# Retiming twelve attention units one by one, and four-block final products, in a hybrid decoder layer

## The chip, the cores and the metric

The kernel runs on one core of a Trainium2 chip. The metric is the device time of one execution in microseconds (us). PE is TensorE, which does the matmuls and turns tiles; DVE (VectorE), ACT (ScalarE) and POOL (GpSimd) do the elementwise work; SP (SyncE) issues most DMAs.

## The reference

One decoder layer on x of 1024 positions by 1024 channels in float32: a mixer of two parallel parts, and then a feed-forward part.

```python
h = rms_norm(x, ln_pre_mix)
proj = h @ w_in                            # 256 pool + 768 q + 768 k + 768 v channels
q, k = rope(q, pos), rope(k, pos)          # 12 heads of 64
pool_out = multi_scale_pool(u_pool, ...)   # window means over 2, 4, 8, 16 positions
attn_out = dilated_attention(q, k, v)      # windows (128,1), (512,4), (2048,16), merged by softmax weights
x = x + rms_norm(concat(pool_out, attn_out) @ w_out, ln_post_mix)
h = rms_norm(x, ln_pre_ffn)
f = (silu(h @ w_gate) * (h @ w_up)) @ w_down
x = x + rms_norm(f, ln_post_ffn)
```

## The kernel before, in words

Each float32 operand of a large product is split in a high part (written by ACT) and a low part, the difference (written by DVE or POOL), and multiplied in three passes. So each matmul operand that is computed on the chip costs an ACT copy and a subtraction. The program falls into three stages: projections, pool mixer and attention (up to about 430 us), then the output projection and the feed-forward part, which is done in seven Strassen-like products (430 to 1090), and its last product with the closing norm (1090 to 1167).

**Units.** Attention is done in six pairs of heads by two halves of the positions, h = 0 and 1, which gives twelve units, u0 to u11 (u0 to u7 are pairs 0 to 3, both halves in turn; u8 and u9 are h = 0 of pairs 4 and 5, u10 and u11 their h = 1). A unit has these steps:

- scores: PE multiplies q by k into a PSUM bank `ps_s`; DVE adds the mask and takes the row's minimum of the scaled scores (L554), ACT takes the exponent and its row sum (L557);
- join, in the function `join`: the two sides of the windows exchange row statistics. DVE forms `ex` for the sides A and B (L577), PE multiplies each by a selection matrix into another `ps_s`, and a row of small DVE steps (L583 to L597) ends in the weights `wv`;
- weighting: 16 multiplies of the exponents `pp` by `wv`, on DVE (L611) or POOL (L613) by the list `wd`;
- turns: PE turns the weighted exponents into `ps_t` (L116), ACT copies the high part `ptr` (L658), DVE subtracts the low part (L659). There are two buffers of `ptr`;
- products: PE multiplies `ptr` by v into `ps_o`; ACT and DVE (L693, L694, L623, L625) finish them into `mix`, which goes to DRAM in `mixd` (L630) and is loaded again as `m` for the output projection (L896).

**Fill.** While a unit's steps wait for DVE, ACT and POOL, PE gets matmuls of projections for later units in between: q and k of one half (`ps_pj`), or v. A finished q or k is rotated (`rope`, L315 to L325): DVE shuffles it (L320) and multiplies by the cosines (L321), an engine chosen by the table (`rq` for q, `rk` for k) multiplies by the sines (L322), another adds (L325), and ACT and DVE spread and split it (L344 to L352). Weights are split at L154 and L158, on DVE or POOL by the list `we`.

**What sets the order.** A step is put on a list with a place, a number in units (`put(steps, lo, hi)`): u + 0.62 is 62% of the way from the start of unit u to the next. A group of steps gets places spread evenly from lo to hi. `emit` sorts the list by place and writes the program in that order. Between those steps PE's matmuls stay in program order. DVE, ACT and POOL are ordered by a scheduler from the same program, with priority for the scores' and turns' helpers and double priority for the join, so their rows move with PE's. SP issues its DMAs in its queue's order, and a DMA that waits for data holds those behind it. The table `PRM` has the places: `h0` and `h1` for units of the two halves, `first` and `last` for u0 and u11, with s0 and s1 for the scores, m for the join, w0 and w1 for the weightings, t0 and t1 for the turns, v0 and v1 for the products. All units of the same half share their places.

**The end.** The class `End` closes the layer. When the last product's sums for all eight blocks of 128 channels are there, PE sums the squares over channels, POOL takes the power -1/2, and PE turns the result into one row factor `rb` in PSUM. Then DVE multiplies each block by the factor and the gain `g4s` (L1418, eight times), DVE or POOL adds the residual `xe` (L1422, eight times), and eight DMAs write 128 KB each.

## Time and profile before

| What | Value |
|---|---|
| median of 3 runs | 1167.78 us (1166.33 to 1168.17) |
| the profiled execution's own time | 1168.91 us |
| its span in the profile | 1167.1 us |
| PE busy | 1136.1 us, 97% of the span |
| DVE busy | 791.6 us, 68% |
| POOL busy | 608.9 us, 52% |
| ACT busy | 543.1 us, 47% |
| mean granted TensorE clock | 0.99 |

The span is the time between the first and the last recorded instruction of one execution; the execution's own time is 1.8 us longer. Busy shares are means over stages: DVE is far fuller in the attention stage than after it. A wait of PE is shown with the engine and line that released it.

### The profile page before, as it was taken

To read this page: it belongs to the slowest core of one execution; us is meant where nothing else is said; L and a number is where in the kernel's file an instruction comes from. 1 tells how busy PE (TensorE), PEld (TensorE's weight loads), DVE (VectorE), ACT (ScalarE), POOL (GpSimd) and SP (SyncE) were. 2 spreads that over 40 slices of the span, in tenths; PEclk is the share of its full clock that TensorE was granted. 3 is DMA by queue.
4 is the path that set the end of the run, shared out by engine and by line. 5 is a ranking of instruction groups with operands and counts; after the bars stand their busy time and mean duration, and the time that the engine had idled before them with its cause. 6 is when DMAs were issued, how large, how long until landed. Compare 5 with 4: busy or idle time off the path is not lost.

```text
span 1167.1 us, 17255 instructions
## 1 busy us (share of the span) xinstructions
PE 1136.1 (97%) x6134; PEld 980.1 (84%) x6134; DVE 791.6 (68%) x1477; ACT 543.1 (47%) x1033; POOL 608.9 (52%) x541
## 2 busy tenths in 40 slices
PE   8999999999998999999999999999999999999996
PEld 6998889989888888888888888888888888888896
DVE  7766778787887675779686665766565465454685
ACT  7356667666566575656433222232232435343420
POOL 0111546565555403160586667777675978656521
PEclk9999999999999999999999999999999999999998
DMA  7315151415124744732233545444535789666542
GB/s 271 102 60 181 37 181 37 159 59 181 55 73 152 281 162 145 280 118 99 87 143 145 185 155 206 163 171 174 188 139 190 266 292 322 207 210 191 178 144 72
DMA packets 85365, 188.51 MB, mean 162 GB/s; under 512 B 8736, under 2 KB 24352, under 8 KB 83872
## 3 DMA queue, kind: packets, MB, share of 16 engines
q1 hardware_dynamic: 84704, 186.90, 46.2%
q8 instruction: 48, 0.79, 0.3%
q10 hardware_dynamic: 576, 0.52, 0.1%
q14 instruction: 37, 0.30, 0.1%
HBM read 134.44 MB, written 52.95 MB: 161 GB/s over the span
## 4 chain that ended last, share of the span: by engine, by line
PE 80%; DVE 8%; ACT 4%; DMA 3%; issue 3%; POOL 1%; SPq 0%; ACTq 0%; POOLq 0%; DVEq 0%
PE ps_pj L113 28%; PE ps_o L113 22%; PE ps_s L113 20%; PE ps_t L113 8%; PE ps_t L116 2%; ACT pp L557 1%; DMA mixd<-mix 1%; DVE z L1041 1%; DVE z L1040 1%; DMA m<-mixd 1%; DMA b<-in_w_out_dram 1%; DVE k L345 1%; DVE whl L158 1%; ACT whl L154 1%; DMA xraw<-in_xT_dram 1%
## 5 line engine op out<-in xcount | busy, mean ns | idle before, releaser
L113 PE MATMUL ps_pj<-x,whl 128*128 128x512 f32 x480 | 145.9, 418 | 0.0
L1225 POOL TENSOR_TENSOR fw<-rw,fw 128x512 fp32r<-128x512 f32 x74 | 102.6, 1414 | 62.9 <-ACT fw L1223 62.9
L613 POOL TENSOR_SCALAR pp<-pp,wv 128x256 f32<-128x256 f32 (+1 forms) x156 | 72.0, 480 | 104.9 <-DVE wv L597 52.1
L113 PE MATMUL ps_o<-tT,fw 128*128 128x512 f32 x504 | 118.1, 390 | 0.0
L158 POOL TENSOR_TENSOR whl<-wraw,whl 128x512 fp32r<-128x512 f32 x50 | 66.5, 1350 | 90.4 <-ACT whl L154 61.0
L113 PEld LDWEIGHTS ps_o<-tT,fw 128*128 128x128 f32 x504 | 94.6, 188 | 20.3
L557 ACT ACTIVATE pp<-pp,sx 128x128 f32<-128x128 f32 (+1 forms) x192 | 89.3, 468 | 30.0 <-DVE sx L554 29.4
L113 PEld LDWEIGHTS ps_pj<-x,whl 128*128 128x128 f32 x480 | 87.4, 194 | 10.3 <-POOL whl L158 0.4
L1225 POOL TENSOR_TENSOR whl<-rw,whl 128x512 fp32r<-128x512 f32 x42 | 62.5, 1511 | 58.0 <-ACT whl L1223 58.0
L1223 ACT ACTIVATE fw<-rw 128x1024 fp32r<-128x1024 f32 x37 | 38.5, 1058 | 100.7 <-DVE rw L1191 42.4
L113 PE MATMUL ps_pj<-whl,x 128*128 128x256 f32 x528 | 80.3, 293 | 0.0
L1367 POOL TENSOR_TENSOR op<-rw,op 128x512 fp32r<-128x512 f32 x38 | 60.6, 1594 | 35.5 <-ACT op L1366 34.2
L659 DVE TENSOR_TENSOR ptr<-ps_t,ptr 128x512 fp32r<-128x512 f32 (+1 forms) x84 | 56.2, 669 | 26.4 <-ACT ptr L658 25.8
L113 PEld LDWEIGHTS ps_pj<-whl,x 128*128 128x128 f32 x528 | 70.7, 196 | 0.5 <-DVE whl L158 0.2
L322 POOL TENSOR_TENSOR rsw<-rsw,sinr 128x512 f32<-128x512 f32 x20 | 26.2, 1309 | 84.7 <-DVE rsw L320 84.7
L658 ACT ACTIVATE ptr<-ps_t 128x512 fp32r<-128x512 f32 (+1 forms) x84 | 48.4, 576 | 40.6 <-PE ps_t L116 39.4
L1366 ACT ACTIVATE op<-rw 128x1024 fp32r<-128x1024 f32 x38 | 40.2, 1060 | 56.3 <-PE ps_t L113 32.2
L113 PE MATMUL ps_o<-ptr,v 128*128 128x128 f32 (+1 forms) x472 | 58.6, 258 | 4.8 <-DVE ptr L659 4.8
L113 PE MATMUL ps_pj<-b,fw 128*128 128x512 f32 x264 | 62.3, 392 | 0.0
L113 PEld LDWEIGHTS ps_o<-ptr,v 128*128 128x128 f32 x472 | 52.6, 164 | 8.8 <-DVE ptr L659 5.9
L113 PEld LDWEIGHTS ps_pj<-b,fw 128*128 128x128 f32 x264 | 49.6, 188 | 10.9
L113 PE MATMUL ps_s<-k,qh 128*128 128x128 f32 (+1 forms) x192 | 53.6, 291 | 0.3 <-DVE sx L554 0.2
(302 smaller groups left out, 2914.9 us busy)
## 6 DMA issues: line engine op xcount, KB each, us to landing
rw<-bd SPq DMA_DIRECT2D x77, 256.0 KB, 4.5
v<-vd SPq DMA_DIRECT2D x22, 512.0 KB, 4.9
rw<-wsd SPq DMA_DIRECT2D x44, 256.0 KB, 4.0
rw<-in_w_gate_dram SPq DMA_DIRECT2D x20, 512.0 KB, 3.6
rw<-in_w_up_dram SPq DMA_DIRECT2D x20, 512.0 KB, 4.5
bd<-p SPq DMA_DIRECT2D x33, 256.0 KB, 2.9
rw<-in_w_down_dram SPq DMA_DIRECT2D x33, 256.0 KB, 4.4
fw<-in_w_down_dram SPq DMA_DIRECT2D x16, 512.0 KB, 4.1
```

The costliest lines, as they stand in the source:

```text
L113: return tc.keep_in_program_order(nc.tensor.matmul(*a, **k))
L116: return tc.keep_in_program_order(nc.tensor.transpose(dst, src, by))
L158: eng.tensor_tensor(dst[:, 1, at:at + w], src[:, at:at + w], dst[:, 0, at:at + w].bitcast(F32), ALU.subtract)
L322: eng[0].tensor_tensor(s, s, sinr[:, sl], ALU.mult)
L557: nc.scalar.activation(pt[:, j, lo:], pt[:, j, lo:], AF.Exp, bias=sx[:, 0, side, j, hd, 0:1], scale=-1.0, accum_out=sx[:, 0, side, j, hd, ...
L613: nc.gpsimd.tensor_scalar(pv, pv, un.wv[:, side, j, hd:hd + 1], 1.0, op0=ALU.mult, op1=ALU.mult)
L658: nc.scalar.activation(ptr[:, 0, :w], t[:, :w], AF.Copy)
L659: nc.vector.tensor_tensor(ptr[:, 1, :w], t[:, :w], ptr[:, 0, :w].bitcast(F32), ALU.subtract)
L1223: nc.scalar.activation(w[n][:, :, 0], raw[n], AF.Copy)
L1225: low[0] = nc.gpsimd.tensor_tensor(w[n][:, i, 1], raw[n][:, i], w[n][:, i, 0].bitcast(F32), ALU.subtract)
L1366: nc.scalar.activation(w[:, :, 0], raw, AF.Copy)
L1367: nc.gpsimd.tensor_tensor(w[:, 0, 1], raw[:, 0], w[:, 0, 0].bitcast(F32), ALU.subtract)
```

## The change

The table `PRM` gets new numbers throughout, and a new entry `du`: for each unit, offsets that are added to the places of its scores, join, weightings, turns and products. The work of the attention stage stays the same in kind and count, and PE issues the same matmuls, in another order. Four parts of the work go to another engine or another shape:

- `rk` moves the sine multiply of the ten k rotations in the fill from POOL to DVE, and `r0` moves one multiply of the first pair from DVE to POOL;
- `wd` puts one weighting more of each unit on DVE (4 in place of 3 of 16);
- `we` puts two weight splits on DVE that POOL did and one on POOL that DVE did;
- at the end, for the second half of positions, ACT multiplies each block of y by its gain `g4s` as soon as the block is summed. DVE then multiplies four blocks at once by the row factor (`times`), and two blocks at once get the residual (`plus`), the first two of them on POOL as two instructions. Four DMAs of 256 KB take the place of eight of 128 KB.

`dealt` with an empty `cut`, `pb` at 0 and `pe` at 1 change nothing here; `need` and `did` are assertions made while the program is written.

```diff
- 'we': (1, 1, 1, 0, 0, 0, 0, 0, 0, 0, 1, 1),
+ 'we': (0, 0, 0, 0, 0, 1, 0, 0, 0, 1, 1, 1),
- 'pm': (0.92, (0.78, 0, 0), (0.84, 1, 0), (0.99, 0, 1), (1.05, 1, 1)),
+ 'pm': (0.9242, (0.76, 0, 0), (0.85679, 1, 0), (1.02476, 0, 1), (1.05, 1, 1)),
- 'rk': (0, 0),
- 'r0': (1, 1),
+ 'rk': (1, 0),
+ 'r0': (0, 1),
- 'wd': (0, 1, 1, 0, 0, 0, 0, 0, 0, 0, 1, 0, 0, 0, 0, 0),
+ 'wd': (0, 1, 1, 0, 0, 0, 0, 1, 0, 1, 0, 0, 0, 0, 0, 0),
+ 'du': {...
+        1: {'t1': -0.0014, 'm': -0.0422, 's1': 0.0048, 'w0': -0.0401, 'v1': -0.0144},
...
@@ units
         g.update(**(G["first"] if u == 0 else {}), **(G["last"] if u == 11 else {}))
+        g.update({k: g[k] + d for k, d in G["du"].get(u, {}).items()})
@@ class End
+            if self.h:
+                nc.scalar.activation(src, src, AF.Copy, scale=g4s[:, d:d + 1])
...
             def add(d):
...
-                i = nc.vector.scalar_tensor_tensor(yd, yd, g4s[:, d:d + 1], box["rb"], op0=ALU.mult, op1=ALU.mult)
-                eng = nc.gpsimd if at_end and d in (0, 2, 4) else nc.vector
...
-                i = eng.tensor_tensor(yd, yd, self.x[d][:, lo:hi], ALU.add)
...
+            def times(n):
+                yd = yblock("%d2" % (n + 1))[:, :, lo:hi]
+                pin(nc.vector.tensor_tensor(yd, yd, box["rb"][:, None].to_broadcast([P, 4, hi - lo]), ALU.mult))
+            def plus(n, i, eng, queue, each):
+                yd, xd = yblock("%d2" % (n + 1))[:, i:i + 2, lo:hi], self.x4[n][:, i:i + 2, lo:hi]
+                for k in range(0, 2, each):
+                    o = eng.tensor_tensor(yd[:, k:k + each], yd[:, k:k + each], xd[:, k:k + each], ALU.add)
...
+                queue.dma_start(out[at:at + 2 * P, 512 + lo:512 + hi].rearrange("(d p) t -> p d t", p=P), yd)
...
+            sums = ((1, 0, nc.gpsimd, nc.scalar, 1), (1, 2, nc.vector, nc.sync, 2), (0, 0, nc.vector, nc.scalar, 2),
+                    (0, 2, nc.vector, nc.sync, 2))
```

The order in which DVE gets its instructions moves with the places. At the join of u1, before, DVE's order is as follows. `ps_o_1251` and `low_1335` belong to a product, `ps_pj_1229` to a projection, `ex` to the join, `ptr` to turns; L659, L694, L320, L321 and L577 are the lines named above.

```order
L659 TENSOR_TENSOR ptr_1317<-ps_t_1312,ptr_1317 128x512
L694 TENSOR_TENSOR ps_o_1251<-ps_o_1251,low_1335 64x512
L320 STREAM_SHUFFLE rsw_1348<-ps_pj_1229 128x512
L321 TENSOR_TENSOR rco_1349<-ps_pj_1229,cosr_271 128x512
L577 TENSOR_TENSOR ex_1377<-sx_1110,qdA_290 128x64
L659 TENSOR_TENSOR ptr_1365<-ps_t_1360,ptr_1365 128x512
L625 TENSOR_TENSOR mix_1252<-ps_o_1251,mix_1252 64x512
```

In the changed kernel, whose lines stand 30 further down in this part (L607 is the former L577, L724 the former L694), the same place reads:

```order
L689 TENSOR_TENSOR ptr_1318<-ps_t_1313,ptr_1318 128x512
L607 TENSOR_TENSOR ex_1364<-sx_1076,qdA_290 128x64
L350 STREAM_SHUFFLE rsw_1349<-ps_pj_1249 128x512
L351 TENSOR_TENSOR rco_1350<-ps_pj_1249,cosr_271 128x512
L724 TENSOR_TENSOR ps_o_1241<-ps_o_1241,low_1337 64x512
L613 TENSOR_TENSOR em_1370<-ps_s_1365,qdA_290 128x64
```

The join's second `ex` moved from behind three instructions of other work to ahead of them.

A little later, among the products of u1, DVE's order before is as follows. L351 and L352 spread the finished q of the fill.

```order
L554 ISA pp_1637,sx_1478<-ps_s_1656,mA_286 128x256
L554 ISA sx_1478 128x1
L351 CAST qh_1587<-rco_1589 64x512 x2
L577 TENSOR_TENSOR ex_1732<-sx_1478,qdB_292 128x64
L352 TENSOR_TENSOR ql1_95<-rco_1589,qh_1587 64x512 x2
L659 TENSOR_TENSOR ptr_1670<-ps_t_1665,ptr_1670 128x512
```

And in the changed kernel, with L381 and L382 for L351 and L352:

```order
L584 ISA pp_1641,sx_1476<-ps_s_1657,mA_286 128x256
L584 ISA sx_1476 128x1
L689 TENSOR_TENSOR ptr_1671<-ps_t_1666,ptr_1671 128x512
L724 TENSOR_TENSOR ps_o_1514<-ps_o_1514,low_1680 64x512
L607 TENSOR_TENSOR ex_1763<-sx_1476,qdA_290 128x64
L381 CAST qh_1589<-rco_1591 64x512 x2
L382 TENSOR_TENSOR ql1_95<-rco_1591,qh_1589 64x512 x2
```

The subtraction that makes the next `ptr` moved from behind the four instructions of L351 and L352 to ahead of them.

On SP, where the last of `mix` of the first half goes to DRAM and is loaded again, the order before is the following (`m02` and `m03` are the loads of `m`, `vd` is v on its way through DRAM, `wraw` a weight).

```order
L896 DMA m00_4546<-mixd_75 128x2x1024
L896 DMA m01_4548<-mixd_75 128x2x1024
L630 DMA mixd_75<-mix_4254 128x1024
L896 DMA m03_4575<-mixd_75 128x2x1024
L150 DMA wraw_4725<-in_w_out_dram 128x1024
L472 DMA vd_77<-vs_4531 128x2x512
L896 DMA m02_4581<-mixd_75 128x1024
```

In the changed kernel:

```order
L937 DMA m00_4533<-mixd_75 128x2x1024
L937 DMA m01_4535<-mixd_75 128x2x1024
L180 DMA wraw_4595<-in_w_out_dram 128x1024
L660 DMA mixd_75<-mix_4255 128x1024
L180 DMA wraw_4725<-in_w_out_dram 128x1024
L937 DMA m03_4576<-mixd_75 128x2x1024
L937 DMA m02_4574<-mixd_75 128x1024
L502 DMA vd_77<-vs_4550 128x2x512
```

The load `m02` moved ahead of the store `vd`, and one weight's load ahead of the store of `mix`.

## The prediction

> **What bounds the kernel now.** I read the page first, where PE has by far the largest share of the span, then the windows by stage, then PE's waits, and then the timeline at the longest of them. The windows' columns are the stretch, its length, busy time of PE, PEld, DVE, ACT and POOL (with instructions), the granted clock, the DMA share and GB/s.

> ```profile
> 100.00:430.00 330.00, 314.39 (x2092) 288.12 (x2091) 257.20 (x759) 212.92 (x571) 162.57 (x208) 0.98 0.37 123
> 430.00:1090.00 660.00, 659.68 (x2975) 544.08 (x2975) 413.34 (x491) 259.25 (x339) 410.09 (x290) 1.00 0.53 188
> 1090.00:1168.00 78.00, 66.05 (x434) 60.30 (x432) 52.95 (x90) 18.69 (x26) 21.12 (x17) 0.93 0.37 123
> ```

> PE bounds everything. Between 430 and 1090 us it idles 0.3 us, so nothing is to be had there. In the attention stage it idles 330.00 - 314.39 = 15.6 us, in the last stage 12. The matmuls stay the same ones, so the time can change only through these idle times and the clock. The attention's idle time has few owners:

> ```profile
> PE ps_o L113 <- DVE ptr L659: 4.8, 4, 1.5
> PE ps_s L113 <- DVE ex L577: 4.4, 3, 2.5
> PE ps_t L116 <- POOL pp L613: 3.0, 2, 2.7
> PE ps_pj L113 <- DMA m<-mixd: 2.2, 2, 1.6
> ```

> Each row is total, number and longest. PE waits for joins (`ex`), for turned weights (`ptr`), for weightings on POOL, and for `m`. There is a second price. After four of these waits come stretches at half clock. The one behind u1's join, and then a stretch of the same length that follows no wait:

> ```profile
> 122.70:126.10 3.40, 3.40 (x11) 2.64 (x10) 3.22 (x10) 1.98 (x4) 0.31 (x1) 0.50 0.00 0
> ...
> 140.00:143.40 3.40, 3.40 (x26) 3.40 (x26) 2.53 (x8) 3.35 (x10) 1.22 (x1) 1.00 0.11 43
> ```

> At clock 0.50, 3.4 us do the work of 1.7, so such a stretch costs about 1.7 us. The others lie behind the join at 305.84, the product at 342.81 and the turn at 374.45 (below).

> **The change part by part.**

> *Join of u1.* DVE first, then the join on PE and what POOL did at the time:

> ```profile
> 119.52 0.73 DVE L320 STREAM_SHUFFLE rsw<-ps_pj 128x512 f32<-128x512 f32 x1
> ...
> 120.15 0.66 DVE L321 TENSOR_TENSOR rco<-ps_pj,cosr 128x512 f32<-128x512 f32 x1
> ...
> 120.39 1.26 POOL L322 TENSOR_TENSOR rsw<-rsw,sinr 128x512 f32<-128x512 f32 x1 [8.93 <-DVE rsw L320]
> ...
> 120.74 0.99 DVE L577 TENSOR_TENSOR ex<-sx,qdA 128x64 f32<-128x64 f32 x1
> ...
> 121.78 0.43 PE L113 MATMUL ps_s<-ex,ls 128*128 128x64 f32 x2 [1.48 <-DVE ex L577]
> ```

> The second `ex` stands behind other work, and takes 0.99 us beside a POOL multiply. The order now puts it ahead of L320, L321 and L694, so DVE could do it from 119.5. PE has three matmuls of a projection fewer ahead of the join, so I leave 0.2 us of the wait: -1.3 (0.9 to 1.5). The half-clock stretch at 122.7 goes with it: -1.7 (0 to 1.7).

> *Products of u1, and one of u3.*

> ```profile
> 147.06 0.63 PE L113 MATMUL ps_o<-ptr,v 128*64 128x256 f32 x5 [0.42 <-DVE ptr L659]
> ...
> 147.71 1.12 DVE L351 CAST qh<-rco 64x512 fp32r<-64x512 f32 x2
> ...
> 149.01 1.40 DVE L352 TENSOR_TENSOR ql<-rco,qh 64x512 fp32r<-64x512 f32 x2
> ...
> 150.44 0.69 DVE L659 TENSOR_TENSOR ptr<-ps_t,ptr 128x512 fp32r<-128x512 f32 x1
> ...
> 151.19 0.79 PE L113 MATMUL ps_o<-ptr,v 128*64 128x128 f32 x7 [1.52 <-DVE ptr L659]
> ...
> 204.43 1.66 DVE L345 TENSOR_TENSOR k<-rcl,k 64x512 fp32r<-64x512 f32 x1
> ...
> 206.12 0.69 DVE L659 TENSOR_TENSOR ptr<-ps_t,ptr 128x512 fp32r<-128x512 f32 x1
> ...
> 206.87 0.33 PE L113 MATMUL ps_o<-ptr,v 128*64 128x256 f32 x1 [1.45 <-DVE ptr L659]
> ```

> In u1 PE idles 0.42 + 1.52 = 1.94 us, since `ptr` queues behind 2.5 us of q's spreading. The new order makes `ptr` first: -1.8. The products stand a little closer behind their turns now, so up to 0.5 of new waiting is the other end (-1.9 to +0.5). In u3, `ptr` stands behind the 1.66 us of L345; the new order spreads k well before: -1.3 of 1.45 (-1.45 to 0).

> *Join of u7.*

> ```profile
> 302.12 0.22 DVE L577 TENSOR_TENSOR ex<-sx,qdB 128x64 f32<-128x64 f32 x1
> ...
> 304.44 1.26 POOL L322 TENSOR_TENSOR rsw<-rsw,sinr 128x512 f32<-128x512 f32 x1 [6.19 <-DVE rsw L320]
> ...
> 304.78 1.00 DVE L577 TENSOR_TENSOR ex<-sx,qdA 128x64 f32<-128x64 f32 x1
> ...
> 305.84 0.43 PE L113 MATMUL ps_s<-ex,ls 128*128 128x64 f32 x2 [2.51 <-DVE ex L577]
> ```

> Here the second `ex` stays behind the same other work. What goes is the POOL multiply beside it, which is a k's and moves to DVE, behind. By the row of the other side, `ex` alone takes 0.22: 1.00 - 0.22 = -0.8. The remaining 1.7 us and the half-clock stretch stay. Ends: -4.2, wait and stretch both, to +0.5.

> At both joins `ex`, with two operands in SBUF, ends 0.08 us after POOL's multiply does (121.73 and 121.65; 305.78 and 305.70). [...]

> *Unchanged places.* The longest wait for `ptr` behind the small steps of u7's join (342.81), the join of u9, and the first turn of u9, which waits for POOL:

> ```profile
> 342.81 0.62 PE L113 MATMUL ps_o<-ptr,v 128*64 128x256 f32 x5 [1.39 <-DVE ptr L659]
> ...
> 374.45 0.68 PE L116 MATMUL ps_t<-idt,pp 128*128 128x128 f32 x4 [2.70 <-POOL pp L613]
> ```

> The first gets POOL's work sooner and DVE's later; I take 0 (-3.1 to +1.5). In the second POOL has one addition of a rotation (L325) more ahead of the weightings, and PE more matmuls ahead of the turn: +0.3, between -1.3 and +1.3, one POOL instruction like L322 below either way.

> *Pool means and the load of m.*

> ```profile
> 103.41 1.28 PE L113 MATMUL ps_o<-band,u 128*128 128x144 f32 x10 [0.95 <-DVE mix L627]
> ...
> 392.74 0.96 PE L113 MATMUL ps_pj<-m,whl 128*128 128x512 f32 x3 [0.54 <-DMA m<-mixd]
> ...
> 396.49 0.73 PE L113 MATMUL ps_pj<-m,whl 128*128 128x512 f32 x2 [1.65 <-DMA m<-mixd]
> ```

> The two `pool_means` come earlier and apart from the product that holds their bank: -0.7 (-0.95 to 0). On SP, `m02` no longer stands behind the store `vd`, but a weight's load came ahead of the store of `mix`: -1.0 (-2.2 to 0).

> *Work moved to DVE.* Its price by the rows of the attention stage, the last column before the bar being the count, then busy and mean ns:

> ```profile
> L322 POOL TENSOR_TENSOR rsw<-rsw,sinr 128x512 f32<-128x512 f32 x20 | 26.2, 1309 | 84.7 <-DVE rsw L320 84.7
> ...
> L321 DVE TENSOR_TENSOR rco<-ps_pj,cosr 128x512 f32<-128x512 f32 x20 | 13.5, 673 | 0.0
> ...
> L611 DVE TENSOR_SCALAR pp<-pp,wv 128x256 f32<-128x256 f32 x15 | 6.6, 481 | 0.2
> ...
> L158 DVE TENSOR_TENSOR whl<-wraw,whl 128x1024 fp32r<-128x1024 f32 x5 | 6.4, 1287 | 1.0 <-ACT whl L154 0.9
> ```

> No row shows the sine multiply on DVE. The bounds are L321 with 0.67 and the contended L345 with 1.66 us; POOL is busy in 162.57 of 330 us, half of the time, and loses this work itself, so I take 0.8. Ten of these, twelve weightings at 0.48 and one net split at 1.29 make 8 + 5.8 + 1.3 = 15 us (14 to 24). DVE goes from 257 to 272 of 330 us, 78% to 82%. It is no bound by share, but a fuller queue makes `ptr` and `ex` later, and some units' joins and products stand nearer behind their inputs than before. For such fresh waits I put +2.5, one like 1.5 us and a share of a half-clock stretch; ends 0 and +8, two like u7's join with a stretch each (2 x 4.2).

> *The end.*

> ```profile
> 1158.02 0.87 DVE L1418 SCALAR_TENSOR_TENSOR y<-y,g4s,ps_pj 128x256 f32<-128x256 f32 x2 [1.56 <-PE ps_pj L116]
> ...
> 1163.86 0.42 DVE L1422 TENSOR_TENSOR y<-y,xe 128x256 f32<-128x256 f32 x1
> ...
> L1441 DVE TENSOR_TENSOR y<-ps_o,y 128x512 f32<-128x512 f32 x3 | 1.9, 675 | 0.0
> ...
> L1422 DVE TENSOR_TENSOR y<-y,xe 128x512 f32<-128x512 f32 x8 | 8.9, 1162 | 0.0
> ```

> DVE works from 1158.02 to 1164.28. A sum over 128x512 with one PSUM operand takes 0.675, so I estimate 1.2 for `times` over 128x1024; two of these and three `plus` of 128x512 at 0.68 make 2.4 + 2.0 = 4.4 us against 6.26, -1.8. The ACT scaling falls beside the sums. A last transfer of twice the size gives back some 0.2: -1.6. At worst the three `plus` take the 1.16 of such sums in the first half, 1.4 more in all, and the transfer 0.7 more: +0.5. At best a `times` takes no more than two of the present multiplies (0.87): -1.6 - 2 x 0.33 - 0.2, about -2.5.

> *Sum.* -1.3 - 1.7 - 1.8 - 1.3 - 0.8 + 0 + 0.3 - 0.7 - 1.0 + 2.5 - 1.6 = -7.4. The profiled execution took 1168.9 us, 1.1 more than the median, so it would take 1161.5 now, and a median run 1160.4.

> [...]

> **The rivals.**

> *Every long wait goes.* Each unit's own places could also clear u7's and u9's waits with their three stretches: 1.7 + 1.4 + 2.7 + 3 x 1.7 = 10.9 less, and no fresh wait, 1160.4 - 10.9 = 1149.5, or about 1151 with part of the fresh ones. Against it: at u7's join DVE's order is the same.

> *DVE becomes the bound of the joins and products.* The ten sine multiplies read two SBUF operands, as L345 and `ex` do, which took 1.66 and 1.00 beside POOL. If each meets a split or a sum on POOL, DVE's extra work is 24 us, and `ptr` comes late. It decides once DVE's queue ahead of `ptr` is over 1 us longer in some four units. Four more waits of 1.5 with a stretch of 1.7 each are 12.8 in place of 2.5, and the 3.1 of u1's and u3's products don't come: 1160.4 + 10.3 + 3.1 = 1173.8. For it: DVE is 78% busy, and PE's waits for DVE are the largest now. Against it: POOL gives up as many instructions as DVE gets, and so meets fewer of DVE's others. [...]

> *The waits only move.* Each wait that goes comes back in another unit: only the end's gain is left with some of `m`, 1167.8 - 1.6 = 1166.2. For it: PE's matmuls between the steps are the same number, so a unit that gets more cover takes it from another.

> **How the numbers follow.** About 0.2%, 2.3 us, is what a measurement can tell from no change: 1165.4 to 1170.1. Forecast (1156 to 1165) 0.47, every wait gone 0.14, waits only move 0.20, of which a third gains more than 0.2%, DVE the bound 0.19. Faster is 0.47 + 0.14 + 0.07 = 0.68, the same 0.13, slower 0.19. The range for 8 in 10 runs from 1151 to 1171, which leaves out most of the DVE rival and part of the best one; the forecast's own is 1156 to 1165.

> **What would show it.** In the changed profile: no wait of over 0.5 us for `ex` near 120 and no half clock behind it; no wait for `ptr` near 150 and 206; a wait of about 1.7 for `ex` near 304 with `ex` at 0.2; the end's DVE work about 4.4 us. DVE in the attention stage near 272 us. It is wrong if waits for `ptr` and `ex` together are over 9 us again, or there are more than three half-clock stretches.

## The result, and the profile after

The changed kernel takes 1153.73 us, the median of 4 runs (1153.31 to 1156.6), against 1167.05 us for the kernel before in 4 runs (1165.22 to 1168.17): 13.3 us less, a ratio of 0.9893 with a 95% interval of 0.9871 to 0.9914. The profiled execution took 1153.31 us; its span is 1151.4, against 1167.1 before.

So the time lies 2.3 us below the forecast's own range of 1156 to 1165, inside the wide one of 1151 to 1171, and above the rival in which every long wait goes (1149.5 to 1151).

The windows by stage of the changed kernel (columns as in the prediction). Its attention stage ends 14.6 us earlier, so the cuts stand at 415.4 and 1075.4 where they stood at 430 and 1090:

```profile
100.00:415.40 315.40, 308.01 (x2087) 284.31 (x2087) 261.42 (x776) 213.65 (x566) 140.86 (x184) 0.99 0.37 129
415.40:1075.40 660.00, 659.18 (x2972) 543.81 (x2971) 415.20 (x492) 259.99 (x339) 410.58 (x289) 1.00 0.53 188
1075.40:1152.00 76.60, 65.79 (x434) 60.20 (x432) 50.36 (x72) 25.52 (x38) 20.46 (x16) 0.95 0.38 125
```

In the attention stage PE idles 7.4 us in place of 15.6, although DVE is busy for 261 of 315 us (83%) in place of 257 of 330 (78%). PE's waits of the changed kernel (L607 was L577, L643 was L613, L689 was L659, L584 was L554):

```profile
PE ps_t L146 <- POOL pp L643: 3.7, 3, 3.0
...
PE ps_s L143 <- DVE ex L607: 1.5, 1, 1.5
...
PE ps_o L143 <- DVE ptr L689: 1.3, 3, 0.6
...
PE ps_s L143 <- DVE sx L584: 0.3, 1, 0.3
PE ps_pj L143 <- POOL whl L188: 0.3, 1, 0.3
```

The wait for `m` has no row any more, and neither has u1's join, where both `ex` now end ahead of PE's need (the second waits for ACT itself):

```profile
117.12 0.23 DVE L607 TENSOR_TENSOR ex<-sx,qdA 128x64 f32<-128x64 f32 x1 [0.30 <-ACT pp L587]
...
117.98 0.55 PE L143 MATMUL ps_s<-ex,ls 128*128 128x64 f32 x4
```

One wait for `ex`, u7's, and one for the weighting in u9 are left of the long ones:

```profile
297.31 0.43 PE L143 MATMUL ps_s<-ex,ls 128*128 128x64 f32 x2 [1.55 <-DVE ex L607]
...
363.49 0.68 PE L146 MATMUL ps_t<-idt,pp 128*128 128x128 f32 x4 [3.00 <-POOL pp L643]
```

u9's wait has the pattern that u7's last product had before (shown below, where the prediction is gone through): on DVE the join's small steps are slow beside POOL's work (`wv` takes 0.90 us, against 0.17 at u7's last product, at 332.29), and on POOL a split and a rotation's addition (L355) stand ahead of the weighting.

```profile
361.00 0.90 DVE L627 TENSOR_TENSOR wv<-nm,dd 128x16 f32<-128x16 f32 x1
...
359.36 2.51 POOL L188 TENSOR_TENSOR whl<-wraw,whl 128x512 fp32r<-128x512 f32 x2
...
361.82 1.26 POOL L355 TENSOR_TENSOR rco<-rco,rsw 128x512 f32<-128x512 f32 x1
```

Of the four half-clock stretches in the attention stage one is left, behind the wait of u9; the place behind u1's join now runs at full clock:

```profile
365.40:368.80 3.40, 3.40 (x18) 3.40 (x18) 3.31 (x9) 0.89 (x4) 3.40 (x7) 0.50 0.99 398
122.70:126.10 3.40, 3.40 (x18) 2.56 (x17) 3.20 (x11) 0.93 (x3) 0.79 (x2) 1.00 0.00 0
```

At the end DVE's work is 4.5 us, where it was 6.3:

```profile
1143.10 2.35 DVE L1469 TENSOR_TENSOR y<-y,ps_pj 128x1024 f32<-128x1024 f32 x2 [1.30 <-PE ps_pj L146]
1145.37 2.24 DVE L1474 TENSOR_TENSOR y<-y,xe 128x512 f32<-128x512 f32 x3
```

### The profile page after: what moved, and what is told of

Its sections match the earlier page's. It is cut to its first block, busy times and chain, and to the rows that moved or that the text cites. A ratio compares the mean times of both kernels' runs of the same rounds, so it can differ in the third digit from the quotient of the medians.

```text
span 1151.4 us, 17214 instructions
## 1 busy us (share of the span) xinstructions
PE 1128.8 (98%) x6134; PEld 976.3 (85%) x6134; DVE 795.2 (69%) x1481; ACT 552.5 (48%) x1045; POOL 589.8 (51%) x517
## 3 DMA queue, kind: packets, MB, share of 16 engines
HBM read 134.44 MB, written 52.95 MB: 163 GB/s over the span
## 5 line engine op out<-in xcount | busy, mean ns | idle before, releaser
L143 PE MATMUL ps_pj<-x,whl 128*128 128x512 f32 x480 | 142.0, 409 | 0.0
L643 POOL TENSOR_SCALAR pp<-pp,wv 128x256 f32<-128x256 f32 (+1 forms) x144 | 69.8, 503 | 118.2 <-DVE wv L627 70.2
L188 POOL TENSOR_TENSOR whl<-wraw,whl 128x512 fp32r<-128x512 f32 x48 | 63.8, 1349 | 59.5 <-ACT whl L184 54.9
L689 DVE TENSOR_TENSOR ptr<-ps_t,ptr 128x512 fp32r<-128x512 f32 (+1 forms) x84 | 56.0, 666 | 13.7 <-ACT ptr L688 13.1
L143 PEld LDWEIGHTS ps_pj<-b,fw 128*128 128x128 f32 x264 | 49.6, 188 | 10.9
L143 PE MATMUL ps_s<-k,ql 128*128 128x128 f32 (+1 forms) x192 | 52.9, 284 | 0.0
```

Of the source, the lines that this page charges most:

```text
L143: return tc.keep_in_program_order(nc.tensor.matmul(*a, **k))
L188: eng.tensor_tensor(dst[:, 1, at:at + w], src[:, at:at + w], dst[:, 0, at:at + w].bitcast(F32), ALU.subtract)
L643: nc.gpsimd.tensor_scalar(pv, pv, un.wv[:, side, j, hd:hd + 1], 1.0, op0=ALU.mult, op1=ALU.mult)
L689: nc.vector.tensor_tensor(ptr[:, 1, :w], t[:, :w], ptr[:, 0, :w].bitcast(F32), ALU.subtract)
```

## Experiments

Theory: the gain is one of order. PE's long waits came from other work standing ahead of the instruction it waited for, on DVE and POOL, and the new places turn these orders round. Rivals: moving work off POOL brings it by itself; or the closing part does; or the common numbers do it and the single units' offsets are small corrections. The kernels ran in four groups, each beside the kernel before on the same chip; its medians there were 1166.43, 1167.13, 1166.65 and 1166.62 us, and the ratios below are to these. A part taken out of the changed kernel also upsets the order that the other numbers were made for, so what a part is worth depends on the rest: such differences don't add up.

**The parts alone and taken away.** `tail_only` is the kernel before with the new class `End`.

> The kernel before with the new closing class alone (gain on ScalarE, times, plus, four DMAs). If the closing part is worth what the two traces show from the last sum of y to the end (12.65 us before, 11.55 after), the time falls by 1.1 us, to about 1166.0. By the prediction's own term it falls by 1.6, to 1165.4. If the end is hidden by something else, nothing changes.

Measured: 1166.38 us in 11 runs, ratio 0.9999 (0.9991 to 1.0008). `old_tail` is the opposite, the changed kernel with the old `End`.

> The changed kernel with the closing part of before. If the new closing part is worth the 1.1 us that the traces show: 1154.8. If, as the run of it alone had it, it is worth nothing: 1153.7.

Measured: 1154.86 us (1154.65 to 1158.82), ratio 0.9907 (0.9892 to 0.9922), 1.1 us above the changed kernel, but the intervals of the two overlap. The profiles agree with each other: from the wait for the last `p` to the end of the span there are 11.7 us before (1155.44 to 1167.1), 11.4 in `old_tail` (1141.64 to 1153.0), 10.7 in `tail_only` (1153.90 to 1164.6) and 10.6 after (1140.78 to 1151.4). So the closing part is worth some 0.7 to 1.0 us of span, which the times can't settle. Of the larger figure 0.26 us is clock: in the profile of before alone the turn of the row factor (1157.29) fell into half clock and took 0.69 us, against 0.43 in the three others.

`engines_only` is the kernel before with the engine choices, at the old places.

```diff
-        'we': (1, 1, 1, 0, 0, 0, 0, 0, 0, 0, 1, 1),
+        'we': (0, 0, 0, 0, 0, 1, 0, 0, 0, 1, 1, 1),
-        'rk': (0, 0),
-        'r0': (1, 1),
+        'rk': (1, 0),
+        'r0': (0, 1),
-        'wd': (0, 1, 1, 0, 0, 0, 0, 0, 0, 0, 1, 0, 0, 0, 0, 0),
+        'wd': (0, 1, 1, 0, 0, 0, 0, 1, 0, 1, 0, 0, 0, 0, 0, 0),
```

> The kernel before with the engine choices alone (rk, r0, wd, we), all places old. Theory 'order': the gain comes from the places, so the moved work by itself gives at most the 0.8 us at u7's join and costs new waits for ptr and ex behind a fuller DVE queue: 1166 to 1171 us. Rival 'POOL relieved': most of the gain comes from GpSimd leaving VectorE's operands alone: 1157 to 1161 us, with two or three of the four half-clock stretches gone.

Measured: 1166.59 us in 12 runs, ratio 1.0004 (0.9994 to 1.0014), as the theory had it: POOL's relief alone brings nothing. At u7's join `ex` takes 0.21 us and PE waits 1.73, 0.8 less than before:

```profile
305.52 0.21 DVE L577 TENSOR_TENSOR ex<-sx,qdA 128x64 f32<-128x64 f32 x1
...
305.79 0.43 PE L113 MATMUL ps_s<-ex,ls 128*128 128x64 f32 x2 [1.73 <-DVE ex L577]
```

The waits for `ptr` fall too, from 4.8 to 1.3 us. But new waits for weightings and for scores (2.4 us, from 0.2) stand elsewhere, and in all PE still idles 13.9 us in the attention stage. The rows of the weightings:

```profile
PE ps_t L116 <- POOL pp L613: 4.3, 3, 2.7
...
PE ps_t L116 <- DVE pp L611: 1.8, 4, 0.7
```

`order_only` is the changed kernel with the four old engine choices.

> The changed kernel with the old engine choices (rk, r0, wd, we): new places, du and closing part only. Theory 'order': most of the gain stays, 1155 to 1159 us; the join of u7 waits 2.4 instead of 1.55 us and its half-clock stretch is back. Rival 'POOL relieved': 1162 us or more.

Measured: 1158.11 us (1155.93 to 1160.33), ratio 0.9936 (0.9924 to 0.9949). Of the 13.3 us, 8.3 remain without any of the moved work. Its profile has u7's wait at 2.33 us, as expected, but without the half-clock stretch that was expected too, and waits for `ptr` of 3.5 us in all against 1.3:

```profile
298.81 0.43 PE L143 MATMUL ps_s<-ex,ls 128*128 128x64 f32 x2 [2.33 <-DVE ex L607]
...
PE ps_o L143 <- DVE ptr L689: 3.5, 4, 1.6
```

Two of the four choices, undone singly in the changed kernel, tell which matters. `rk_back` sets `'rk': (0, 0)`:

> The changed kernel with the ten sine multiplies of k back on POOL. Theory 'POOL's instruction beside the join's ex was in the way': u7's join waits about 2.4 instead of 1.55 us and gets its half-clock stretch in most runs, 1156 to 1158 us. Rival 'the multiply only loads DVE' (the prediction's slower case): 1151 to 1153 us, since DVE loses 8 us of work.

Measured: 1159.28 us (1159.01 to 1160.95), ratio 0.9935 (0.9923 to 0.9947), 1 us more than expected: undoing this one choice costs as much as undoing all four. u7's join waits 2.31 us there, with a half-clock stretch (mean clock of the profile 0.993, against 0.995 in the changed kernel), and waits for `ptr` are 4.4 us in all. `wd_back` puts the old weighting list in:

> The changed kernel with the old list of weightings on DVE, one fewer per unit. If the weighting list matters by POOL's time before the first turns: u9's wait stays at 3.0, others appear for POOL, 1154.5 to 1157 us. If it only loads DVE: 1152 to 1153.5 us.

Measured: 1154.19 us (1154.06 to 1154.28), ratio 0.9888 (0.9876 to 0.9901). It lies between the two expectations, and the interval holds the changed kernel's ratio: no difference is shown. u9's wait is 3.00 us there too.

**More on DVE.** `rq_dve` goes on in the same direction, and puts q's ten sine multiplies on DVE too.

```diff
- 'rq': (0, 0),
+ 'rq': (1, 0),
```

> The changed kernel with q's ten sine multiplies on DVE too (rq like rk). If POOL's instructions beside DVE's are what makes DVE late, u9's join loses its collision with the multiply (small steps of 0.9 and 1.2 us there fall to 0.2), and the time falls to 1150 to 1153 us. If DVE's own load is what matters (the prediction's slower rival, now with 16 + 8 us more than before the change): 1155 us or more, with new waits for ptr.

Measured: 1176.82 us (1175.75 to 1179.32), ratio 1.0088 (1.0074 to 1.0102). So this is where the prediction's slower rival lies, one step further. But not in its way: PE hardly waits for `ptr` (0.6 us in all), it waits for weightings on POOL. The first theory missed as well: u9's small steps still take 1.25 and 1.17 us, now beside the split and the addition that POOL keeps, and the wait there is 3.19 us.

```profile
PE ps_t L146 <- POOL pp L643: 17.9, 5, 4.8
```

One of them on DVE, POOL and PE:

```profile
126.27 0.25 DVE L625 RECIPROCAL nm<-nm 128x16 f32<-128x16 f32 x1
126.50 0.69 DVE L724 TENSOR_TENSOR ps_o<-ps_o,low 64x512 f32<-64x512 f32 x1
127.12 0.72 DVE L350 STREAM_SHUFFLE rsw<-ps_pj 128x512 f32<-128x512 f32 x1
127.74 0.67 DVE L351 TENSOR_TENSOR rco<-ps_pj,cosr 128x512 f32<-128x512 f32 x1
128.33 0.66 DVE L627 TENSOR_TENSOR wv<-nm,dd 128x16 f32<-128x16 f32 x1
...
127.69 3.02 POOL L188 TENSOR_TENSOR whl<-wraw,whl 128x512 fp32r<-128x512 f32 x2 [5.49 <-ACT whl L184]
130.69 1.49 POOL L643 TENSOR_SCALAR pp<-pp,wv 128x256 f32<-128x256 f32 x3
...
131.26 1.12 PE L146 MATMUL ps_t<-idt,pp 128*128 128x128 f32 x4 [4.74 <-POOL pp L643]
```

The join's last step `wv` stands behind a product and a rotation (L724, L350, L351), and on POOL a weight split of 3.0 us stands ahead of the weightings. In the changed kernel `wv` comes right behind the reciprocal there, and POOL's split behind the weightings.

**The places.** `no_du` is the changed kernel with `'du': {}`.

> The changed kernel with du empty: all units of a half share their places again, with the new common numbers. If the single units' offsets carry the gain: 1160 to 1166 us, waits for ex and ptr of over 1 us back in three or more units. If the common numbers and the engine choices carry it: 1154 to 1157 us.

Measured: 1170.82 us (1168.39 to 1174.67), ratio 1.0042 (1.0028 to 1.0056). The offsets, some of a few thousandths of a unit, are worth 17 us, more than the whole change, and 5 more than the first expectation allowed. The waits that come back are not those expected: PE waits 13.7 us in all for weightings on POOL, twice 4.66 (L620 is the weighting there, L165 the split).

```profile
PE ps_t L123 <- POOL pp L620: 13.7, 5, 4.7
...
187.08 1.22 DVE L604 TENSOR_TENSOR wv<-nm,dd 128x16 f32<-128x16 f32 x1
...
187.01 2.49 POOL L165 TENSOR_TENSOR whl<-wraw,whl 128x512 fp32r<-128x512 f32 x2 [5.02 <-ACT whl L161]
...
190.44 1.32 PE L123 MATMUL ps_t<-idt,pp 128*128 128x128 f32 x4 [4.66 <-POOL pp L620]
```

It is the same picture as in `rq_dve`: on DVE `wv` behind a shuffle and a multiply of a rotation, on POOL the split first and the weightings behind it. `du_2_4` keeps only the offsets of u2 and u4, where the two waits are.

> The changed kernel with the offsets of u2 and u4 alone. Without any offsets PE waited 4.66 us twice for POOL's weightings, in u2 and u4, with half-clock stretches behind both. If the offsets work place by place, these two waits go with their 1.7 us each (and a further stretch): 1170.8 - 2 x 6.4 = 1158 us, the waits of the other units staying as without offsets. If the offsets work only as a whole: 1165 us or more.

Measured: 1160.78 us (1158.94 to 1163.85), ratio 0.9949 (0.9933 to 0.9965). So the offsets mostly work place by place: the two waits shrink to pairs of 0.78 and 0.72 to 0.73 us, and those of the other units (1.73 at u7's join, 3.46 in u9) are as without offsets. `two_v0` keeps only two numbers, the places of the products in these units, which turn POOL's order there round.

```diff
+ 'du': {2: {'v0': 0.0155}, 4: {'v0': 0.0085}},
```

> The changed kernel with only two of the offsets left: the products of u2 start 0.0155 units later and those of u4 0.0085 units later; these alone turn GpSimd's order there round, from weight split before weightings to weightings before weight split. Theory 'the order of a split and the weightings on GpSimd makes the two waits of 4.66 us': both go with their half-clock stretches, 1158 to 1161 us, as with all offsets of u2 and u4 (1160.8). Rival 'the offsets act by the cover they give PE's waits': so small a shift does little, 1168 us or more.

Measured: 1162.92 us (1160.33 to 1164.06), ratio 0.9971 (0.9959 to 0.9983), 2 us more than expected, but 7.9 below `no_du`. The order in `two_v0` at the first of the two places (the weighting is L546 there, the split L91, `wv` L530; the window ends in the split):

```profile
184.46 0.15 DVE L530 TENSOR_TENSOR wv<-nm,dd 128x16 f32<-128x16 f32 x1
...
184.79 6.12 POOL L546 TENSOR_SCALAR pp<-pp,wv 128x256 f32<-128x256 f32 x12 [4.29 <-DVE wv L530]
190.87 1.28 POOL L91 TENSOR_TENSOR whl<-wraw,whl 128x512 fp32r<-128x512 f32 x1
```

The weightings come first, and the two waits of 4.66 are two pairs of 0.84 and 0.72 and of 0.79 and 0.72. So these two places are shown as the cause of the two waits. They act on two queues, though: on DVE `wv` now comes ahead of the rotation and takes 0.15 us in place of 1.22, and on POOL the weightings come ahead of the split. How much of the 4.66 us each is worth was not separated.

`old_common` is the opposite of `no_du`: offsets, engines and closing part new, the common numbers old.

> The changed kernel with the old common numbers of places; offsets du, engine choices and closing part are the new ones. If the offsets alone carry the order's gain: 1154 to 1157 us. If offsets and common numbers only work together: 1161 us or more, with waits for POOL's weightings or DVE's ptr of over 1 us in three or more units.

Measured: 1167.63 us in 11 runs, ratio 1.0005 (0.9995 to 1.0016). The offsets only work on the numbers they were made for; a wait of 2.14 us for `ex` stands at u1's join, and POOL's weightings cost 5.2 us.

**An attempt on the wait that is left.** `u9_late` moves u9's first turns and products later, so that more matmuls lie between its join and its first turn.

```diff
-        9: {'m': 0.0183, 'w1': -0.0315, 't1': -0.0102, 's1': -0.0286},
+        9: {'m': 0.0183, 'w1': -0.0315, 't1': -0.0102, 's1': -0.0286, 't0': 0.25, 'v0': 0.1},
```

> The changed kernel with u9's first turns 0.25 units and its first products 0.1 units later, so that some 3 us more matmuls lie between u9's join and its first turn. Theory 'a wait costs itself and, when it fills enough of a 3.4 us window, a half-clock stretch': the 3.0 us wait for the weighting on POOL goes, and with it the only stretch in the attention stage: 3.0 + 1.7 less, about 1149 us, mean clock 0.997 or more in most runs. Rival 'the wait moves on': u9's products or u10's join wait instead, 1152 to 1154 us.

Measured: 1156.3 us (1152.77 to 1158.46), ratio 0.9904 (0.9889 to 0.992). The rival was right, and the result a little worse than it said. The wait is gone and comes back at u10's scores, 1.19 and 2.60 us, where PE needs a `ps_s` that DVE has not read yet (L487 is the former L554):

```profile
369.93 0.39 PE L46 MATMUL ps_s<-k,qh 128*128 128x256 f32 x1 [1.19 <-DVE sx L487]
...
373.70 0.57 PE L46 MATMUL ps_s<-k,qh 128*128 128x256 f32 x1 [2.60 <-DVE sx L487]
```

My reading is that DVE is behind by those 3 us here, whichever wait shows it; no run shows this by itself. No kernel tried beats the changed one.

## Why the prediction was right, and where its size was off

The direction, most places of the gain and the wide range held; the fall was 13.3 us where 7.4 were summed up, 1.8 times as much, and the time fell below the forecast's own range. The signs named for it held: no long wait at u1's join and products, 1.55 us at u7's with `ex` at 0.22, DVE's closing work at 4.5 us, one half-clock stretch. Step by step, with the two profiles beside the terms:

| Step | Predicted | In the profiles |
|---|---|---|
| u1's join | -1.3 | -1.5 (1.48 to none) |
| its half-clock stretch | -1.7 | -1.7 |
| u1's products | -1.8 | -1.9 (0.42 and 1.52 to none) |
| u3's product | -1.3 | -1.45 |
| u7's join | -0.8 | -0.96 (2.51 to 1.55) |
| its stretch | 0 | -1.7 |
| u7's last product and the turn behind | 0 | -1.35 (1.39 and 0.31 to 0.35) |
| their stretch | 0 | -1.7 |
| u9's join | 0 | -0.4 |
| u9's first turn | +0.3 | +0.3 (2.70 to 3.00) |
| pool means | -0.7 | -0.6 (0.95 to 0.34) |
| load of `m` | -1.0 | -2.2 (0.54 and 1.65 to none) |
| fresh waits | +2.5 | +2.3, six of 0.34 to 0.56 |
| the end | -1.6 | -1.0 |

The right column makes 13.9 of the 15.7 us between the two spans; the rest was not taken apart, and a new wait of 0.50 us at 456.83, behind the attention stage, goes against it. The profiled execution of before took 1168.91 us, 1.9 more than the median of its four runs, so the medians stand only 13.3 apart.

Most waits were read rightly, to 0.2 us, since an order of instructions and the durations of before give them. Four steps were mis-sized. First, "The remaining 1.7 us and the half-clock stretch stay" at u7's join: the wait stayed, at 1.55 us, and the stretch did not. I took a stretch to belong to a wait; in the profiles it goes by windows of time, as the last section shows. That it stayed away in this profile is partly luck: in `old_tail` the same wait, 1.52 us, has it. So is the 1.7 us credited at u1's join: in `tail_only` the old wait of 1.50 us has none. Second, for u7's last product "I take 0". POOL's instructions stand otherwise there now. Before, POOL worked through a multiply, a split and an addition without a pause, beside DVE's small steps of the join:

```profile
339.98 0.95 DVE L593 TENSOR_TENSOR de<-dd,sx 128x32 f32<-128x32 f32 x1 [0.30 <-ACT dd L591]
340.96 1.19 DVE L594 TENSOR_TENSOR nm<-de 128x16 f32<-128x16 f32 x1
342.07 0.68 DVE L659 TENSOR_TENSOR ptr<-ps_t,ptr 128x512 fp32r<-128x512 f32 x1
...
337.10 1.28 POOL L322 TENSOR_TENSOR rsw<-rsw,sinr 128x512 f32<-128x512 f32 x1 [5.40 <-DVE rsw L320]
338.34 2.54 POOL L158 TENSOR_TENSOR whl<-wraw,whl 128x512 fp32r<-128x512 f32 x2
340.84 1.28 POOL L325 TENSOR_TENSOR rcl<-rco,rsw 128x512 f32<-128x512 f32 x1
```

In the changed kernel, on DVE and POOL:

```profile
331.56 0.19 DVE L623 TENSOR_TENSOR de<-dd,sx 128x32 f32<-128x32 f32 x1 [0.30 <-ACT dd L621]
331.79 0.18 DVE L624 TENSOR_TENSOR nm<-de 128x16 f32<-128x16 f32 x1
...
329.94 1.29 POOL L355 TENSOR_TENSOR rcl<-rco,rsw 128x512 f32<-128x512 f32 x1
```

The steps take 0.19 and 0.18 us in place of 0.95 and 1.19. With the multiply gone from POOL, its addition ends at 331.23, ahead of them. The moved multiply alone does not do it: with it on DVE the wait is still 1.29 us in `engines_only` and in `no_du`; with it back on POOL in the new order it is 1.91 us (`rk_back`). It takes both. Third, the load of `m` was credited with half and all of it went, but not all by the new order: `tail_only`, where SP has the old order, waits 0.51 us for `m` in all. The last load lands 6.5 us behind its issue there, and 7.8 in the profile of before, so some 1.7 of the 2.2 us is the pace of the transfers in one execution. Fourth, the end gained 0.6 less than said: DVE's part was right (4.5 us against an estimate of 4.4), but 3.8 us lie behind DVE's last instruction (1147.61 to 1151.4) where there were 2.8 (1164.28 to 1167.1), so the transfers of 256 KB took back 1.0, not 0.2; the 0.2 was my estimate, and no row of before gave it. Of the 1.0 that is left 0.26 is the clock of the row factor's turn, as said above.

Work moved to DVE was sized well: L352 takes 0.75 us against 0.8 assumed, and the rows of the moved work make 7.5 + 5.8 + 1.3 = 14.6 us against 15. (A row did show the sine multiply on DVE: the four of the first pair before, L322, at 683 ns each.) But the prediction took DVE's load to rise by all of it, to 272 us, and over the same part of the work it rose by 4, from 257.20 to 261.42. Other rows grew shorter, such as the 20 of L345 (855 to 758 ns each) and the 12 of L594 (431 to 260); the rest of this was not taken apart.

```profile
L352 DVE TENSOR_TENSOR rsw<-rsw,sinr 128x512 f32<-128x512 f32 x10 | 7.5, 748 | 0.1
```

The rival that a fuller DVE queue would cost more than it brings did not hold for this step; the next one is slower, as it said, by other waits (`rq_dve`). The rival that every long wait goes was half right: u7's two stretches went and u9's wait stayed. Its sum had a slip: 1149.5 still holds the 2.5 us of fresh waits, and without them it is 1147.0. The relief of POOL shows at two places: with no POOL instruction beside them, `ex` at u7 went from 1.00 to 0.22 us, and the two small steps above from 2.14 to 0.37. The prediction counted on the first and did not see the second; what makes DVE's instructions longer there was not tried. What the prediction did not see at all is how much hangs on a few thousandths of a place: at one place in u2 they turn a wait of 4.66 us into 0.84 and 0.72, and this was in none of the rivals.

## What to carry to other kernels

In a kernel bound by one engine, list that engine's long waits and see what stands ahead of the awaited instruction in its own queue; the change's effect is the sum over these places, and another engine's busy share says little (DVE went from 78% to 83% here while the time fell by 1.1%). Numbers that set an order act by jumps: the parts of this change give nothing (engines alone), little (the end), or a loss (common numbers without offsets), and a gain of 13.3 us together, so judge such numbers by the order that comes out, not by their size. An instruction moved to a fuller engine can pay when a short step on a chain that is waited for no longer stands beside it (here `ex` at u7, 1.00 to 0.22 us), and the same move once more can lose all of it (`rq_dve`, 1176.82 us).

## What the runs showed of the hardware

```profile
119.26:122.67 3.41, 1.93 (x17) 1.71 (x16) 3.41 (x7) 1.17 (x4) 2.20 (x2) 1.00 0.00 0
122.67:126.08 3.41, 3.41 (x11) 2.67 (x10) 3.23 (x10) 1.98 (x4) 0.34 (x1) 0.50 0.00 0
```
```profile
122.10:125.51 3.41, 1.91 (x11) 1.58 (x11) 3.34 (x8) 0.96 (x2) 2.55 (x2) 1.00 0.00 0
125.51:128.92 3.41, 3.41 (x21) 2.91 (x19) 3.21 (x9) 1.36 (x4) 0.00 (x0) 1.00 0.00 0
```

With 1.4 to 1.7 us of a window idle it went either way in the attention stage of the six: half clock followed 1.48 us (before, from 119.26), 1.52 (`old_tail`, from 295.50) and 1.69 (`old_common`, from 246.24), and none followed 1.44 (before, from 204.58), 1.57 (`old_common`, from 119.94) and 1.60 (`two_v0`, from 298.71). All eleven windows there with 1.70 us or more idle (1.70 to 3.41) were followed by half clock. A longer wait that a boundary divides went either way too. In the changed kernel u9's wait of 3.00 us leaves 1.49 and 1.50 us idle in two windows (from 358.58 and 361.99), and the stretch follows. In `engines_only` u9's wait of 2.72 us leaves 1.29 and 1.42 us idle in two windows, and no stretch follows:

```profile
367.04:370.45 3.41, 2.12 (x18) 1.91 (x16) 3.34 (x6) 0.84 (x1) 2.73 (x3) 1.00 0.25 79
370.45:373.86 3.41, 1.99 (x17) 1.92 (x18) 2.38 (x4) 1.16 (x2) 3.41 (x8) 1.00 0.96 281
373.86:377.27 3.41, 3.41 (x26) 3.41 (x25) 2.85 (x6) 3.15 (x6) 3.41 (x6) 1.00 0.80 276
```

So a wait of 1.5 to 3 us cost itself and, in some of the profiles, a stretch behind it: 1.7 us more, an estimate from 3.41 us at clock 0.50. Much of the spread between runs of one kernel goes with the clock: the changed one ran at a mean clock of 0.995 in 1153.3 to 1153.8 us and once at 0.992 in 1156.6. Two windows with less idle time also preceded half clock in the attention stage of the six. One, of 0.94 us (`old_common`, from 102.88), lies among the pool's matmuls of 144 columns. The other, of 0.91 us (`rq_dve`, from 130.35), was at half clock itself, behind a window that was idle throughout. What sets the clock there was not tried.
